# Moving the convolution's transposes of a gated-DeltaNet mixer from TensorE to VectorE and DRAM

## The chip, the cores and the metric

The kernel runs on one core of one Trainium2 chip. The metric is the device time of one execution in microseconds; the time before is the median of three runs. One further execution was taken with the hardware profiler, and all rows of the profile come from it.

## The reference

One decoder layer over 256 tokens of width 2048, in float32. Before and after a mixer stands a half-step SwiGLU FFN (width 5632), then a gated per-layer embedding and a last RMSNorm. The change lies in the mixer:

```python
proj = n @ w_in                       # q|k|v|z (1024 each), a, b, and q|k|v of the other 8 heads
qkv = silu(causal_depthwise_conv(proj[..., :3072], conv_w))     # 4 taps along time
q_c, k_c, v_c = split(qkv, 3)                                   # 8 heads of 128 each
q_c = l2_norm(q_c) * 128 ** -0.5;  k_c = l2_norm(k_c)           # over each head's 128 columns
o_dn = chunk_gated_delta_rule(q_c, k_c, v_c, g, beta)           # chunks of 64 tokens
o_dn = rms_norm(o_dn, dn_out_norm) * silu(z_dn)
o_sb = stick_breaking_attention(q_sb, k_sb, v_sb)
h = h + concat(o_dn, o_sb) @ w_out
```

The delta rule solves a unit lower triangular system for each head and chunk and then sweeps the chunks in order.

## The kernel before

**Matmuls.** Every float32 weight tile is loaded by SP into `raw` (four buffers of 128x1024, a pair of 128x512 tiles), rounded by ScalarE to `whi` (L68) and its remainder put by VectorE into `wlo` (L69), three buffers each. A product is three matmuls, hi*hi, hi*lo and lo*hi (L103 to L105), so a pair is twelve matmuls over the two halves of 128 tokens. `next_weights` keeps two pairs split ahead of the one in use.

**The mixer.** The input projection goes through fourteen blocks of 512 columns, in the order `W_IN_ORDER`, eight weight pairs each (112 pairs in all), and the output projection through four blocks. Blocks 2, 3 are k of the two head groups (four heads each), 0, 1 are q, 4, 5 are v; 8 to 13 belong to the attention and 6, 7 are z. A block's result (`pj`, two PSUM tiles, tokens on the partitions) is scaled by ScalarE into SBUF (`nat`, L663).

**Order of the work.** Side work is written as generators in three lanes. After each weight pair `lanes.step()` advances the first generator of every lane to its next `yield`: CONV holds the convolutions one after another, and later the attention's transposes and the gates; CHAIN holds the decays and then the delta rule of each head group; STICK the attention. Within this program order a planner in the framework may let an instruction of an engine go ahead of a blocked one; each engine then runs its queue in order. SP's queue holds the weight loads and the side work's transfers together.

**The convolution** (`conv_silu`) needs channels on the partitions and time along the row. `transpose_pair` turns `nat` on TensorE into PSUM (`tr_p`, L672, eight 128x128 transposes a block); ScalarE multiplies by the last tap (L801), VectorE adds the three others (L803) and ScalarE applies SiLU. `transpose4` (L679) turns the result back (`tr_b`, eight a block), and from PSUM ScalarE copies v (L818), or squares and sums q and k for their norms (`rnorm`, L785), GpSimd takes the power, and for k VectorE scales (L831); four transposes for each half of the tokens turn the scaled k again (`tr_kn`). The head group's chain starts its products `kk` (L876) when all three of its blocks are done (`ready`).

**The chain** (`chain`) forms `kk`, sends the diagonal blocks through DRAM, solves 32 rows one after another on VectorE (L904 and L906, dependent on each other), sends the solution back through DRAM, and runs some ten short products on TensorE, the last being `op1` (L956 into `op`), one step of the lane apart. Norms and a power follow; `gate` multiplies by SiLU of z, transposes, and makes `dnT`, the output projection's input. The second head group's `dnT` is used from the seventh pair of the first output block on.

**The other way to transpose** is there already (`transposed`, L163 to L177): VectorE transposes 32x32 blocks of a 128x512 tile, twice; SP stores both to a DRAM scratch tile (`scr`) and loads them with the block rows and columns exchanged, in four loads. It serves the norms' blocks, the FFN's inner activations, the attention's q and k, and the gate. It yields four times: after the block transposes, after the stores, after the loads, and once more.

Of the kernel before, what the change touches and what calls it, by code (L numbers as in the profile page):

```python
# [16 lines left out]
P = 128  # L17
# [13 lines left out]

W_IN_ORDER = (2, 0, 4, 3, 1, 5, 8, 10, 12, 9, 11, 13, 6, 7)
EPS = 1e-6
# [4 lines left out]
def block_kernel(ctx, tc, a, out):  # L38
# [14 lines left out]

    lanes = Lanes(3)
    dr = ctx.enter_context(tc.tile_pool(name="dr", bufs=1, space=bass.MemoryType.DRAM))
# [95 lines left out]
    def split_scaled(hi, lo, src, gain):  # L151
        nc.scalar.activation(hi, src, AF.Copy, scale=gain)
        nc.vector.scalar_tensor_tensor(out=lo, in0=src, scalar=gain, in1=hi.bitcast(F32),  # L153
                                       op0=ALU.mult, op1=ALU.subtract)

    def transposed(src, dst=None):

        scr = dr.tile([P, 2, 4, P], F32, tag="scr", name="scr", bufs=2)  # L160
        tmp = [act.tile([P, 4, P], F32, tag="nat", name="tb", bufs=4) for _ in range(2)]
        for t in range(2):
            nc.vector.transpose(tmp[t].rearrange("p c (j x) -> p c j x", j=4),  # L163
                                src(t).rearrange("p (j c x) -> p c j x", j=4, c=4))
        yield
        for t in range(2):
            nc.sync.dma_start(out=scr[:, t], in_=tmp[t])
        yield
        if dst is None:
            dst = [act.tile([P, 4, P], F32, tag="nat", name="tT", bufs=4) for _ in range(2)]  # L170
        for c in range(4):
            part = slice(32 * c, 32 * c + 32)
            if isinstance(dst, list):
                for t in range(2):
                    nc.sync.dma_start(out=dst[t][part], in_=scr[:, t, c, :].rearrange("(q x) i -> x q i", q=4))
            else:
                nc.sync.dma_start(out=dst[part], in_=scr[:, :, c, :].rearrange("(q x) t i -> x t q i", q=4))  # L177
        yield
        yield
        return dst  # L180

    def norm_block_behind(nT, which, j, tmp):

        hi, lo = nT
        yield
        tT = tmp()
        yield from transposed(lambda t: h[:, t, block(j)], tT)
# [30 lines left out]
    def block(j):  # L218
        return slice(j * NB, (j + 1) * NB)
# [178 lines left out]
    def ffn(n, nT, r, scale, next_norm, stat):  # L398
        xs = picker(*nT)
        late = callable(r)  # L400
        with tc.tile_pool(name="ffn", bufs=1) as fp:
            hTh, hTl = [], []

            def down_input(u, sil, th, tl):
                for t in range(2):
                    nc.vector.scalar_tensor_tensor(out=sil[:, t, :], in0=u[t], scalar=r[:, t:t + 1], in1=sil[:, t, :],
                                                   op0=ALU.mult, op1=ALU.mult)
                yield
                tT = fp.tile([P, 2, 4, P], F32, tag="tT", name="tT")
                yield from transposed(lambda t: sil[:, t, :], tT)  # L410
# [208 lines left out]
def mixer(tc, nc, a, act, mm_ps, mx_ps, accumulate, picker, new_nT, norm_block, sumsq, block, lanes, transposed,  # L619
          nT, r, h, stat, ident, mhalf):  # L620
    xs = picker(*nT)
    C64 = P // 2
    CONV, CHAIN, STICK = 0, 1, 2
    blocks = list(W_IN_ORDER)

    with tc.tile_pool(name="mix", bufs=1) as mp, \
# [32 lines left out]
        def to_sbuf(o, dst=None):  # L659
# [5 lines left out]
            return res  # L665

        def transpose_pair(nat, pr):

            tr = mx_ps("tr_p")
            for q in range(2):  # L670
                for t in range(2):
                    nc.tensor.transpose(tr[:, q * T + t * P:q * T + (t + 1) * P],  # L672
                                        nat[t][:, (2 * pr + q) * P:(2 * pr + q + 1) * P], ident)
            return tr

# [115 lines left out]

        def conv_silu(nat, part, hg):
            y = mp.tile([P, 4 * T + P], F32, tag="cT", name="cT", bufs=3)[:, 0:4 * T]
            trp = [transpose_pair(nat, pr) for pr in range(2)]
            for pr in range(2):
                for q in range(2):
                    c = 2 * pr + q
                    x = trp[pr][:, q * T:(q + 1) * T]
                    yc = y[:, c * T:(c + 1) * T]
                    w = conv[:, part * H + hg * 4 + c, :]  # L800
                    nc.scalar.activation(yc, x, AF.Copy, scale=w[:, 3:4])  # L801
                    for s in (1, 2, 3):
                        nc.vector.scalar_tensor_tensor(out=yc[:, s:], in0=x[:, 0:T - s], scalar=w[:, 3 - s:4 - s],  # L803
                                                       in1=yc[:, s:], op0=ALU.mult, op1=ALU.add)
                    yield
            if part == 0:
                yv = y.rearrange("p (c t x) -> p c t x", c=4, t=2)
                for t in range(2):
                    nc.scalar.activation(knq[hg][t][:, :, 1, :], yv[:, :, t, :], AF.Silu)
                src = lambda c, t: knq[hg][t][:, c, 1, :]  # L810
            else:
                nc.scalar.activation(y, y, AF.Silu)
                src = lambda c, t: y[:, c * T + t * P:c * T + (t + 1) * P]
            yield
            trs = [transpose4("tr_b", lambda c: src(c, t)) for t in range(2)]
            if part == 2:
                for t in range(2):
                    nc.scalar.copy(vn_[hg][:, t], trs[t])  # L818
            else:
                ss = mp.tile([P, 8], F32, tag="ss", name="ss", bufs=2)  # L820
                for t in range(2):
                    rnorm(trs[t], ss, t)
                if part == 0:
                    inv_sqrt(ss, rq[hg])
                else:
                    inv_sqrt(ss, ss)
                    yield
                    yield
                    kns = [kdec[hg], s2("kn1")]
                    for t in range(2):  # L830
                        nc.vector.tensor_tensor(out=v3(kns[t]), in0=v3(trs[t]), in1=bc(ss[:, t * 4:t * 4 + 4]),  # L831
                                                op=ALU.mult)
                    yield
                    yield
                    for t in range(2):
                        tr = transpose4("tr_kn", lambda c: kns[t][:, c * P:(c + 1) * P])
                        nc.scalar.copy(knq[hg][t][:, :, 0, :], v3(tr))
            ready[hg] += 1
            yield

        def dn_block(part, hg):
            nat = to_sbuf(natural(2 * part + hg))
            lanes.add(CONV, conv_silu(nat, part, hg))

# [5 lines left out]
        def chain(hg):  # L850
# [51 lines left out]
            for i in range(1, 32):  # L902
# [3 lines left out]
                nc.vector.tensor_reduce(out=sol[:, :, i:i + 1], in_=pm[:, :, 0:i + 1], axis=AX.X, op=ALU.add)  # L906
                if i % 4 == 3 or i % 2 and lanes.q[CONV]:
                    yield
# [80 lines left out]
            nc.vector.tensor_tensor(out=o[:, 1], in0=op1, in1=o[:, 1], op=ALU.add)  # L989


            coef = mp.tile([P, 8], F32, tag="coef", name="coef", bufs=2)
            for t in range(2):
                rnorm(o[:, t], coef, t)
            nc.vector.tensor_tensor(out=coef, in0=coef, in1=rq[hg], op=ALU.mult)
# [19 lines left out]
        def sb_transposed(nat, dst, part, hg):  # L1015

            if part == 0:
                parts = yield from transposed(lambda t: nat[t])
                qv = dst.rearrange("p (c t q y) -> p t q c y", c=4, t=2, q=4)
                for t in range(2):  # L1020
                    nc.scalar.copy(qv[:, t], parts[t].rearrange("p q (c y) -> p q c y", c=4))
            else:
                yield from transposed(lambda t: nat[t], dst.rearrange("p (t q x) -> p t q x", t=2, q=4))
            sb_ready[hg] += 1
# [78 lines left out]
        def gate(y, hg):  # L1103
            while not chain_done[hg]:
                yield
            for t in range(2):
                nc.vector.tensor_tensor(out=y[t], in0=y[t], in1=o_nat[hg][:, t], op=ALU.mult)
            yT = mp.tile([P, 4 * T + P], F32, tag="cT", name="yT", bufs=3)[:, 0:4 * T] \
                .rearrange("p (t q x) -> p t q x", t=2, q=4)
            yield from transposed(lambda t: y[t], yT)  # L1110
            if hg == 0:
# [101 lines left out]
```

## Time and profile before

| what | value |
|---|---|
| median of 3 runs | 1981.55 us (1981.34 to 1981.57) |
| the profiled execution's own time | 1982.68 us |
| its span, first to last instruction | 1981.0 us |
| mean granted TensorE clock | 0.999 |
| DMA moved | 421.64 MB, mean 213 GB/s |

The span covers the instructions; the 1.7 us between it and the execution's time lie around them. In rows of the profile, L numbers are lines of the kernel, a tile is written `out<-in`, and `128x512 f32` is partitions by elements. The input projection's matmuls start between 708 and 1085 us. PE is TensorE, DVE VectorE, ACT ScalarE, POOL GpSimd, and SPq the queue of SP's transfers.

### The profile page before, as it was taken

The numbers are of one execution on the slowest core, as the hardware profiler recorded it, in microseconds if no ns is written. First come the engines' busy times: TensorE is split into PE (matmuls) and PEld (weight loads), VectorE is DVE, ScalarE is ACT, GpSimd is POOL, SyncE is SP. The second block draws the span as 40 slices with busy tenths as digits, with TensorE's granted clock in tenths as the row PEclk, the third lists the DMA queues.
The fourth block names the chain that finished last, engine by engine and source line by source line (L and its number), as shares of the span: only waits on it lengthen the run. The fifth ranks groups of instructions, "written<-read, shape, count | busy, mean of one in ns | idle before, by whom it ended". The sixth has DMA issues, their size and how long they took to land. (4 is left out here: it accounts for less than half of the span.)

```text
span 1981.0 us, 24832 instructions
## 1 busy us (share of the span) xinstructions
PE 1961.9 (99%) x9022; PEld 1621.5 (82%) x9022; DVE 1507.4 (76%) x1803; ACT 1116.1 (56%) x1441; POOL 30.1 (2%) x46
## 2 busy tenths in 40 slices
PE   9999999999999999999999999999999999999998
PEld 7888888888888888878878888888888888888887
DVE  6878788777887766794786677888787877887655
ACT  6655555555555557654545455665565555655654
POOL 0000000000000000000100000000000000000000
PEclk9999999999999999999999999999999999999999
DMA  9666667756667665555564786665667656665764
GB/s 329 225 222 212 217 209 227 237 186 212 230 215 226 203 210 163 175 179 193 171 206 148 248 269 209 228 230 195 215 217 245 213 192 210 225 225 198 241 206 151
DMA packets 163228, 421.64 MB, mean 213 GB/s; under 512 B 20512, under 2 KB 59424, under 8 KB 162976
## 3 DMA queue, kind: packets, MB, share of 16 engines
q1 hardware_dynamic: 161952, 418.58, 64.2%
q10 hardware_dynamic: 1152, 1.47, 0.2%
q8 instruction: 71, 1.16, 0.2%
q14 instruction: 53, 0.43, 0.1%
HBM read 397.96 MB, written 22.02 MB: 212 GB/s over the span
## 5 line engine op out<-in xcount | busy, mean ns | idle before, releaser
L68 ACT CAST whi<-raw 128x1024 fp32r<-128x1024 f32 (+1 forms) x585 | 614.5, 1052 | 716.8 <-PE u L447 168.4
L69 DVE TENSOR_TENSOR wlo<-raw,whi 128x1024 fp32r<-128x1024 f32 (+1 forms) x585 | 711.9, 1220 | 372.0 <-ACT whi L68 370.9
L446 PE MATMUL g<-wlo,nTh 128*128 128x512 f32 x552 | 216.0, 391 | 0.4 <-DVE wlo L69 0.4
L445 PE MATMUL g<-whi,nTh 128*128 128x512 f32 x552 | 215.2, 391 | 0.7 <-ACT whi L68 0.7
L447 PE MATMUL g<-whi,nTl 128*128 128x512 f32 x552 | 215.8, 391 | 0.0
L445 PE MATMUL u<-whi,nTh 128*128 128x512 f32 x552 | 214.7, 389 | 0.0
L446 PE MATMUL u<-wlo,nTh 128*128 128x512 f32 x552 | 214.7, 389 | 0.0
L447 PE MATMUL u<-whi,nTl 128*128 128x512 f32 x552 | 214.7, 389 | 0.0
L445 PE MATMUL d<-whi,hTh 128*128 128x512 f32 x512 | 199.1, 389 | 1.0 <-ACT hTh L414 1.0
L446 PE MATMUL d<-wlo,hTh 128*128 128x512 f32 x512 | 199.2, 389 | 0.0
L447 PE MATMUL d<-whi,hTl 128*128 128x512 f32 x512 | 199.2, 389 | 0.0
L278 DVE TENSOR_TENSOR slo<-R,shi 128x1024 fp32r<-128x1024 f32 x155 | 189.3, 1222 | 12.6 <-ACT shi L277 2.7
L277 ACT CAST shi<-R 128x1024 fp32r<-128x1024 f32 x155 | 163.3, 1054 | 34.7 <-PE d L313 14.2
L103 PE MATMUL pj<-whi,nTh 128*128 128x512 f32 x448 | 179.5, 401 | 0.0
L104 PE MATMUL pj<-wlo,nTh 128*128 128x512 f32 x448 | 176.0, 393 | 2.3 <-DVE wlo L69 2.1
L105 PE MATMUL pj<-whi,nTl 128*128 128x512 f32 x448 | 175.3, 391 | 0.0
L446 PEld LDWEIGHTS g<-wlo,nTh 128*128 128x128 f32 x552 | 104.0, 188 | 23.7 <-DVE wlo L69 2.1
L445 PEld LDWEIGHTS g<-whi,nTh 128*128 128x128 f32 x552 | 104.0, 189 | 22.6 <-ACT whi L68 1.0
L447 PEld LDWEIGHTS g<-whi,nTl 128*128 128x128 f32 x552 | 104.0, 188 | 21.9 <-DVE nTl L153 0.4
L447 PEld LDWEIGHTS u<-whi,nTl 128*128 128x128 f32 x552 | 103.6, 188 | 21.6
L446 PEld LDWEIGHTS u<-wlo,nTh 128*128 128x128 f32 x552 | 103.6, 188 | 21.5
L445 PEld LDWEIGHTS u<-whi,nTh 128*128 128x128 f32 x552 | 103.6, 188 | 21.5
(301 smaller groups left out, 3028.3 us busy)
## 6 DMA issues: line engine op xcount, KB each, us to landing
raw<-in_w_gu SPq DMA_DIRECT2D x275, 512.0 KB, 4.2
raw<-in_w_down SPq DMA_DIRECT2D x128, 512.0 KB, 3.7
raw<-in_w_in SPq DMA_DIRECT2D x112, 512.0 KB, 3.6
R<-in_w_gu SPq DMA_DIRECT2D x76, 512.0 KB, 5.4
R<-in_w_down SPq DMA_DIRECT2D x48, 512.0 KB, 5.6
scr<-tb SPq DMA_DIRECT2D x74, 256.0 KB, 4.0
raw<-in_w_out SPq DMA_DIRECT2D x32, 512.0 KB, 4.2
raw<-in_w_pg SPq DMA_DIRECT2D x32, 512.0 KB, 4.4
```

Of the source, the lines that this page charges most:

```text
L68: nc.scalar.copy(hi[:, j, :], raw[:, j, :])
L69: nc.vector.tensor_tensor(out=lo[:, j, :], in0=raw[:, j, :], in1=hi[:, j, :], op=ALU.subtract)
L103: nc.tensor.matmul(outs[t], xh[:, c], whi[:, j, :], start=st, stop=False)
L104: nc.tensor.matmul(outs[t], xh[:, c], wlo[:, j, :], start=False, stop=False)
L105: nc.tensor.matmul(outs[t], xl[:, c], whi[:, j, :], start=False, stop=sp)
L277: nc.scalar.copy(hi, w)
L278: nc.vector.tensor_tensor(out=lo, in0=w, in1=hi, op=ALU.subtract)
L445: nc.tensor.matmul(out, xh[:, c], whi[:, j, :], start=st, stop=False, skip_group_check=True)
L446: nc.tensor.matmul(out, xh[:, c], wlo[:, j, :], start=False, stop=False, skip_group_check=True)
L447: nc.tensor.matmul(out, xl[:, c], whi[:, j, :], start=False, stop=sp, skip_group_check=True)
```

## The change

The forward and backward transposes of the convolution go through `transposed`; `tr_kn`, the chain's and the attention's own transposes stay on TensorE. The convolution reads and writes SBUF tiles: a first move brings `nat` into `y`, ScalarE copies it into `x` with the channels' four heads apart (two copies), the taps go from `x` to `y` as before, SiLU is applied, and a second move brings the result back into `x`, from which the norms, the copy of v and the scaling of k read. The blocks of a head group come as k, v, q, and they go into three lanes in turn (CONV and two new ones that are advanced after CHAIN and STICK). q counts as ready after its SiLU; the sum of its squares is needed by the chain's output norm, which waits for `rq_done`.

```diff
-W_IN_ORDER = (2, 0, 4, 3, 1, 5, 8, 10, 12, 9, 11, 13, 6, 7)
+W_IN_ORDER = (2, 4, 0, 3, 5, 1, 8, 10, 12, 9, 11, 13, 6, 7)
...
-    lanes = Lanes(3)
+    lanes = Lanes(5)
...
-        def rnorm(tr, ss, t):
+        def rnorm(src, ss, t):
             for c in range(4):
                 junk = act.tile([P, NB], F32, tag="junk", name="junk", bufs=1)
-                nc.scalar.activation(junk[:, 0:P], tr[:, c * P:(c + 1) * P], AF.Square,
-                                     accum_out=ss[:, t * 4 + c:t * 4 + c + 1])
+                x = src(c)
+                nc.scalar.activation(junk[:, 0:P].rearrange("p (q y) -> p q y", q=4) if len(x.shape) == 3 else
+                                     junk[:, 0:P], x, AF.Square, accum_out=ss[:, t * 4 + c:t * 4 + c + 1])
...
         def conv_silu(nat, part, hg):
+            x = mp.tile([P, 4 * T], F32, tag="sb", name="cx", bufs=6)
             y = mp.tile([P, 4 * T + P], F32, tag="cT", name="cT", bufs=3)[:, 0:4 * T]
-            trp = [transpose_pair(nat, pr) for pr in range(2)]
...
+            yield from transposed(lambda t: v3(nat[t]), y.rearrange("p (t q x) -> p t q x", t=2, q=4))
+            yv = y.rearrange("p (t q c y) -> p t q c y", t=2, q=4, c=4)
+            xv = x.rearrange("p (c t q y) -> p t q c y", c=4, t=2, q=4)
+            for t in range(2):
+                nc.scalar.copy(xv[:, t], yv[:, t])
+            yield
+            for c in range(4):
+                xc, yc = x[:, c * T:(c + 1) * T], y[:, c * T:(c + 1) * T]
...
+                yield
             if part == 0:
                 for t in range(2):
-                    nc.scalar.activation(knq[hg][t][:, :, 1, :], yv[:, :, t, :], AF.Silu)
-                src = lambda c, t: knq[hg][t][:, c, 1, :]
+                    nc.scalar.activation(knq[hg][t][:, :, 1, :], yv[:, t], AF.Silu)
+                src = lambda t: knq[hg][t][:, :, 1, :]
+                ready[hg] += 1
...
             yield
-            trs = [transpose4("tr_b", lambda c: src(c, t)) for t in range(2)]
+
+            back = x.rearrange("p (t q x) -> p t q x", t=2, q=4)
+            yield from transposed(src, back)
...
                 if part == 0:
                     inv_sqrt(ss, rq[hg])
+                    rq_done[hg] = True
+                    return
...
         def dn_block(part, hg):
             nat = to_sbuf(natural(2 * part + hg))
-            lanes.add(CONV, conv_silu(nat, part, hg))
+            lanes.add(CONVS[len(turns) % 3], conv_silu(nat, part, hg))
+            turns.append(part)
...
-                if i % 4 == 3 or i % 2 and lanes.q[CONV]:
+                if i % 4 == 3 or i % 2 and any(lanes.q[x] for x in CONVS):
                     yield
...
+            while not rq_done[hg]:
+                yield
...
-            for part in (1, 0, 2):
+            for part in (1, 2, 0):
                 dn_block(part, hg)
```

`CONVS = (0, 3, 4)`; `turns` counts the blocks. The other callers of `transposed` pass the same data in a view of three dimensions instead of two.

More of the change, by code (lines that the diff above doesn't have):

```diff
@@ L154, in split_scaled, with by_four @@
                                        op0=ALU.mult, op1=ALU.subtract)
+    def by_four(x):
+        return x.rearrange("p (j i) -> p j i", j=4)
     def transposed(src, dst=None):
@@ L186, in norm_block_behind @@
         tT = tmp()
-        yield from transposed(lambda t: h[:, t, block(j)], tT)
+        yield from transposed(lambda t: by_four(h[:, t, block(j)]), tT)
         for kk in range(4):
@@ L409, in down_input @@
                 tT = fp.tile([P, 2, 4, P], F32, tag="tT", name="tT")
-                yield from transposed(lambda t: sil[:, t, :], tT)
+                yield from transposed(lambda t: by_four(sil[:, t, :]), tT)
                 for t in range(2):
@@ L665, in to_sbuf @@
             return res
[L667 to L674, printed above, removed]
         def transpose4(name, src):
@@ L792, in conv_silu @@
         def conv_silu(nat, part, hg):
+            x = mp.tile([P, 4 * T], F32, tag="sb", name="cx", bufs=6)
             y = mp.tile([P, 4 * T + P], F32, tag="cT", name="cT", bufs=3)[:, 0:4 * T]
-            trp = [transpose_pair(nat, pr) for pr in range(2)]
[L795 to L805, printed above, removed]
+            yield from transposed(lambda t: v3(nat[t]), y.rearrange("p (t q x) -> p t q x", t=2, q=4))
@@ new lines, in conv_silu @@
+            yv = y.rearrange("p (t q c y) -> p t q c y", t=2, q=4, c=4)
[5 more added lines that the diff above has]
+                xc, yc = x[:, c * T:(c + 1) * T], y[:, c * T:(c + 1) * T]
+                w = conv[:, part * H + hg * 4 + c, :]
+                nc.scalar.activation(yc, xc, AF.Copy, scale=w[:, 3:4])
+                for s in (1, 2, 3):
+                    nc.vector.scalar_tensor_tensor(out=yc[:, s:], in0=xc[:, 0:T - s], scalar=w[:, 3 - s:4 - s],
+                                                   in1=yc[:, s:], op0=ALU.mult, op1=ALU.add)
+                yield
@@ L817, in conv_silu @@
                 for t in range(2):
-                    nc.scalar.copy(vn_[hg][:, t], trs[t])
+                    nc.scalar.copy(vn_[hg][:, t].rearrange("p (c q y) -> p q c y", c=4, q=4),
+                                   x.rearrange("p (t q c y) -> p t q c y", t=2, q=4, c=4)[:, t])
             else:
@@ L821, in conv_silu @@
                 for t in range(2):
-                    rnorm(trs[t], ss, t)
+                    rnorm(lambda c: back[:, t, c], ss, t)
                 if part == 0:
                     inv_sqrt(ss, rq[hg])
[L825 to L837, printed above, removed]
+                    rq_done[hg] = True
+                    return
+                inv_sqrt(ss, ss)
+                yield
+                yield
+                kns = [kdec[hg], s2("kn1")]
+                for t in range(2):
+                    nc.vector.tensor_tensor(out=kns[t].rearrange("p (c q y) -> p c q y", c=4, q=4), in0=back[:, t],
+                                            in1=ss[:, t * 4:t * 4 + 4].rearrange("p (c o z) -> p c o z", o=1, z=1)
+                                            .broadcast_to([P, 4, 4, 32]), op=ALU.mult)
+                yield
+                yield
+                for t in range(2):
+                    tr = transpose4("tr_kn", lambda c: kns[t][:, c * P:(c + 1) * P])
+                    nc.scalar.copy(knq[hg][t][:, :, 0, :], v3(tr))
             ready[hg] += 1
             yield
+        rq_done = [False, False]
+        turns = []
         def dn_block(part, hg):
             nat = to_sbuf(natural(2 * part + hg))
-            lanes.add(CONV, conv_silu(nat, part, hg))
+            lanes.add(CONVS[len(turns) % 3], conv_silu(nat, part, hg))
+            turns.append(part)
         o_nat = [mp.tile([P, 2, NB], F32, tag="onat", name="onat", bufs=2) for _ in range(2)]
@@ L1017, in sb_transposed @@
             if part == 0:
-                parts = yield from transposed(lambda t: nat[t])
+                parts = yield from transposed(lambda t: v3(nat[t]))
                 qv = dst.rearrange("p (c t q y) -> p t q c y", c=4, t=2, q=4)
@@ L1022, in sb_transposed @@
             else:
-                yield from transposed(lambda t: nat[t], dst.rearrange("p (t q x) -> p t q x", t=2, q=4))
+                yield from transposed(lambda t: v3(nat[t]), dst.rearrange("p (t q x) -> p t q x", t=2, q=4))
             sb_ready[hg] += 1
@@ L1109, in gate @@
                 .rearrange("p (t q x) -> p t q x", t=2, q=4)
-            yield from transposed(lambda t: y[t], yT)
+            yield from transposed(lambda t: v3(y[t]), yT)
             if hg == 0:
```

11 lines of the change are left out of this document (7 added, 4 removed).

## Prediction, made before the changed kernel was run

> **What bounds the kernel now.** I read the page's busy times first, then the windows of the mixer, then the waits there, then single engines in order of time.
>
> ```profile
> span 1981.0 us, 24832 instructions
> PE 1961.9 (99%) x9022; PEld 1621.5 (82%) x9022; DVE 1507.4 (76%) x1803; ACT 1116.1 (56%) x1441; POOL 30.1 (2%) x46
> ```
>
> TensorE is busy for 99% of the span, so an instruction taken off it is worth its time, provided that the weights still come in time. The windows of the mixer say where that proviso is tight (columns: stretch, length, then busy us of each engine, granted clock, DMA share, GB/s):
>
> ```profile
> core 0: us, PE busy (x) PEld busy (x) DVE busy (x) ACT busy (x) POOL busy (x), PEclk, DMA share, GB/s
> 735.00:817.00 82.00, 80.77 (x398) 67.40 (x396) 52.71 (x97) 58.82 (x102) 4.55 (x4) 1.00 0.53 168
> 817.00:890.00 73.00, 71.62 (x337) 58.60 (x336) 67.39 (x138) 41.29 (x79) 4.18 (x2) 1.00 0.58 177
> 890.00:942.00 52.00, 52.00 (x356) 43.45 (x355) 25.17 (x29) 24.97 (x43) 1.32 (x1) 1.00 0.61 200
> ```
>
> The convolutions fill the first two windows. In the second VectorE is busy for 67.39 of 73.00 us, beside TensorE's 71.62; in the third it has half its time free. So TensorE bounds the kernel everywhere, and from 817 to 890 VectorE is close behind. The waits of the mixer (total us, times, longest) agree:
>
> ```profile
> ACT whi L68 <- PE pj L105: 111.5, 64, 4.0
> PE pj L104 <- DVE wlo L69: 2.1, 4, 0.9
> PE tr_b L679 <- ACT cT L812: 1.2, 1, 1.2
> ```
>
> The cast of the weights waits for TensorE to give a buffer back (111.5 us), hardly ever the other way round (2.1 us). The third row is a backward transpose for which TensorE stood idle until the SiLU was done.
>
> **What the change removes.** Each of the six convolution blocks loses eight forward transposes (tr_p) and eight backward ones (tr_b).
>
> ```profile
> L672 PE MATMUL tr_p<-ident,nat x48: 270/272/273, 738.2 to 876.6; 128*128 128x128 f32 x48
> L679 PE MATMUL tr_b<-ident,cT x32: 271/273/327, 756.2 to 891.1; 128*128 128x128 f32 x32
> L679 PE MATMUL tr_b<-ident,knq x16: 270/272/273, 788.4 to 870.3; 128*128 128x128 f32 x16
> ```
>
> That is 48 + 32 + 16 = 96, in twelve groups of eight. The 272 ns are a pipelined duration; what a group takes from the projection shows in TensorE's order of time:
>
> ```profile
> 887.63 0.39 PE L103 MATMUL pj<-whi,nTh 128*128 128x512 f32 x1
> ...
> 890.12 0.39 PE L105 MATMUL pj<-whi,nTl 128*128 128x512 f32 x1
> 890.36 1.03 PE L679 MATMUL tr_b<-ident,cT 128*128 128x128 f32 x8
> 891.15 0.48 PE L103 MATMUL pj<-whi,nTh 128*128 128x512 f32 x1
> 891.46 0.39 PE L104 MATMUL pj<-wlo,nTh 128*128 128x512 f32 x1
> ```
>
> From 887.63 to 890.12 lie twelve matmuls, eleven steps, so one takes 0.227 us and a pair of weight tiles (twelve matmuls) 2.72 us. From 890.12 to 891.46 are two steps, 0.45 us without the group, but 1.34 us went by: a group costs 0.88 us. Twelve make 10.6 us, and the 1.2 us wait for the SiLU goes with them. Gross: **-11.8 us**.
>
> **What it adds on VectorE.** Twelve moves of two 128x512 block transposes. The convolution's multiply-adds stay, now reading SBUF. The groups of the stretch from 817 to 890 (count, busy us, mean ns, idle before and what ended it), and one such pair of block transposes:
>
> ```profile
> L68 ACT CAST whi<-raw 128x1024 fp32r<-128x1024 f32 x23 | 24.2, 1051 | 25.3 <-PE pj L105 24.3 <-ACT cT L801 1.0
> L69 DVE TENSOR_TENSOR wlo<-raw,whi 128x1024 fp32r<-128x1024 f32 x24 | 29.1, 1214 | 2.2 <-ACT whi L68 2.1
> L803 DVE SCALAR_TENSOR_TENSOR cT<-tr_p,conv,cT 128x255 f32<-128x255 f32 (+2 forms) x36 | 14.8, 472 | 0.0
> L904 DVE TENSOR_TENSOR pm<-sol,L 128x16 f32<-128x16 f32 (+30 forms) x31 | 12.8, 411 | 0.9
> L906 DVE TENSOR_REDUCE sol<-pm 128x8 f32<-128x16 f32 (+30 forms) x31 | 9.2, 295 | 0.9
> L831 DVE TENSOR_TENSOR kdec<-tr_b,ss 128x512 f32<-128x512 f32 x1 | 0.7, 692 | 1.6 <-POOL ss L790 1.6
> 888.66 1.30 DVE L163 STREAM_TRANSPOSE tb<-nat 128x512 f32<-128x512 f32 x2
> ```
>
> A move costs VectorE 1.3 us, twelve 15.6 us. Seven fall before the first head group's kk products, where 82.00 - 67.40 = 14.6 us are free: I cost those at nothing. The other five (k backward, v both ways, q both ways, second group) fall into the stretch of the first triangular solve, whose 62 instructions take 22 us. TensorE's time for that stretch shrinks by six groups and its idle 1.4 us, 73.0 - 5.3 - 1.4 = 66.3 us. VectorE needs 67.4 + 5 x 1.3 = 73.9, and 1.6 more where it stands waiting for GpSimd's power (the kdec row), 75.5 us: short by 9.2 us. What cushions it: three sets of split weights, so TensorE has two pairs (5.4 us) in hand while a new one takes 1.05 + 1.21 = 2.3 us, which leaves 3.1 us; and I let 1 us slip into the light stretch after it (q's backward move is needed only by the output norm). 9.2 - 4.1 = 5.1 us of waiting, against 1.4 now: **+3.7 us**. Bounds: -1.4 (all absorbed) and 9.2 + 4.0 (the other idle time of VectorE there, 5.6 - 1.6) - 1.4 = +11.8.
>
> A rule stands against this exchange. The Trainium skill (VectorE: DVE Perf Modes, Rules for kernel authors) says to transpose 128x128 on TensorE if a PSUM destination will do, and calls VectorE's own transpose the fastest for 32x32 blocks only. By that rule VectorE's side of the exchange would be the dearer one; it is the third rival.
>
> **On ScalarE, SP and the queues.**
>
> ```profile
> L1021 ACT COPY sb<-tT x4: 616/618/632, 898.9 to 986.1; 128x512 f32<-128x512 f32 x4
> L167 SPq DMA_DIRECT2D scr<-tb x74: 320/327/1584, 59.5 to 1861.8; - x74
> L177 SPq DMA_DIRECT2D yT<-scr x8: 568/609/614, 1062.2 to 1096.9; - x8
> ACT sb L1021: 0.9, 1
> SPq L167 <- DVE tb L163: 15.6, 12, 3.0
> SPq L177 <- DMA scr<-tb: 7.5, 5, 2.7
> ACT whi L68 <- DMA raw<-in_w_in: 6.4, 3, 5.1
> ```
>
> ScalarE gets twelve copies of 0.62 us, 7.4 us in 155 us of which it is busy 58.82 + 41.29 = 100: nothing. Each copy waits for its transfer with the casts of the weights queued behind it; of the four like it one waited, 0.9 us, under the 3.1 us in hand. Behind it the order of waits is cast, VectorE's subtraction, matmul. SP issues per move two stores (0.33) and four loads (0.61), 3.1 us, and stands in order behind each block transpose and each store's landing, with the next weight loads behind it: at most 3.0 + 2.7 + 3.1 = 8.8 us. The third window holds two such moves and shows TensorE busy for 52.00 of 52.00 us, so I take 0; bounds 0 and +6 (three waits as long as the worst shown, 5.1, less 3.1).
>
> **On the chain of the delta rule.** Lanes advance one step per weight pair, so the yields can be counted. Before, k, q, v take 11, 7 and 7 steps one after another from pair 9 on, and the first group is ready at pair 32. Now k starts at 9, v at 17, q at 25; q's tenth step at 34 makes it ready, and since its lane comes after the chain's, the chain sees it at 35. The first chain ends three pairs later, so the second starts at 77, not 74. Its solve meets a busy convolution lane at other places and wins one pair back: its last product op1 stands after pair 111, not 109, of 112. What follows op1 has no slack today:
>
> ```profile
> L105 PE MATMUL pj<-whi,nTl x448: 387/389/580, 708.9 to 1085.2; 128*128 128x512 f32 x150
> 1076.37 1.05 PE L956 MATMUL op<-vn,AT 128*128 128x128 f32 x8
> 1090.62 0.33 SPq L167 DMA_DIRECT2D scr<-tb  x1
> 1094.92 2.54 SPq L177 DMA_DIRECT2D yT<-scr  x4
> 1100.25 1.14 ACT L1118 CAST dnT<-yT 128x512 fp32r<-128x512 f32 x2
> 1101.75 0.39 PE L103 MATMUL wo<-whi,dnT 128*128 128x512 f32 x1
> DVE zg L1107 <- ACT zg L1137: 1.8, 2, 1.0
> ```
>
> The projection ends at 1085.2 + 0.2 = E. op1 stood at E - 9.0 (three pairs and its own group); now E - 3.6. From op1 to the cast are 23.9 us, through norms, gate, store and load; the cast's first half takes 0.6. That makes E + 20.9, less 1.0 us in which the gate waited for the last z block's SiLU (last row), which now is done before op1's follow-up: E + 19.9. TensorE wants it at 1101.75 = E + 16.3: **+3.6 us**. Bounds: two pairs, 5.4; and 0.9 if the planner puts one pair of the next output block (2.72) into the gap. [...]
>
> **Sum.** -11.8 + 3.7 + 3.6 = -4.5 us against the profiled execution's 1982.68 us (span 1981.0 and 1.7 around it). The median of the runs, 1981.55, lies 1.1 lower; the same difference gives **1977.0 us**.
>
> **The rivals.** Full gain: VectorE catches up by working ahead (in the solve the planner already runs it ahead of the pairs), and one pair covers the gap at the output projection: -11.8 - 1.4 + 0.9 = -12.3, 1969.3 us. For it speaks the free half of the third window; against it, 9.2 us must be found in 66.
>
> Cancelled: VectorE's shortage comes through nearly whole, +11.8, with the tail's 3.6: +3.6, 1985.1 us. For it: instructions of VectorE run in order, and the solve's steps stand ahead of later pairs' subtractions.
>
> Slower, VectorE the bound over both windows: if the first seven moves find their 14.6 us of idle time in the wrong places (it sits where VectorE waits for ScalarE's cast), all 15.6 us lie on the path: -11.8 + 15.6 + 3.6 = +7.4, 1989.0 us. It decides once the added work exceeds what is idle plus 3.1 us of weights in hand. Rows for: 1.30 us a move against 0.88 us a group on TensorE. Against: the cast waits 111.5 us for TensorE. The Trainium skill's rule above would be right here.
>
> Slower by the queue: SP's 8.8 us hold makes weights late. With half of the twelve moves costing 2.0 (5.1 - 3.1): +12 on my sum, 1989 us. Against it: the third window.
>
> **How the numbers follow.** Some 0.2% (4 us) is what a measurement here can tell from no change. My forecast has 0.45; its own range is 1973 to 1981, two thirds of it faster (0.30), the rest within (0.15). Full gain 0.20, faster. Cancelled 0.17, of it 0.12 within and 0.05 slower. VectorE the bound 0.11 and the queue 0.07, slower. Faster 0.50, same 0.27, slower 0.23. The range reaches from 1969.5 (full gain) to 1987.0 (past the cancelled case), leaving the two slower rivals out.
>
> **What would show it.** No tr_p or tr_b on TensorE; 24 more block transposes of 0.65 to 0.7 us; TensorE waiting for wlo some 5 us during the first solve (right), none (full gain) or over 10 (cancelled); TensorE idle 2 to 5 us before the first wo matmul on dnT's second group. I am wrong if ScalarE's cast waits for raw by more than 10 us in the mixer, or if the first wait appears before 817 us.

## The result, and the profile after

The changed kernel takes 2010.42 us (median of 4 runs, 2008.68 to 2011.69) against 1981.56 for the kernel before (4 runs): a ratio of 1.0145, 95% interval [1.0128, 1.0163]. It is 28.9 us slower; the forecast was 4.5 us faster, and the range ended at 1987.0. The profiled execution took 2011.36 us. The page's span and busy times, and then the windows of the mixer (the prediction's stretches and columns):

```profile
span 2009.6 us, 24808 instructions
PE 1960.1 (98%) x8926; PEld 1615.6 (80%) x8926; DVE 1522.9 (76%) x1827; ACT 1120.9 (56%) x1452; POOL 28.6 (1%) x46
```
```profile
735.00:817.00 82.00, 75.82 (x334) 60.40 (x332) 56.84 (x104) 55.61 (x88) 3.09 (x3) 0.98 0.70 218
817.00:890.00 73.00, 58.69 (x236) 46.82 (x237) 63.85 (x130) 35.50 (x71) 3.28 (x2) 0.88 0.73 220
890.00:942.00 52.00, 44.89 (x293) 36.13 (x292) 26.72 (x38) 25.13 (x47) 0.00 (x0) 0.97 0.66 195
```

The edit is as announced: 96 matmuls fewer, 24 instructions of VectorE more, 15.5 us. But from 817 to 890 TensorE is busy for 58.69 us instead of 71.62, VectorE for less than before, and the granted clock is 0.88. No engine is full; they wait for each other. The waits from 735 to 960, first TensorE's and ScalarE's, then SP's queue in the changed kernel, and last SP's queue in the kernel before:

```profile
PE pj L103 <- ACT whi L68: 16.1, 5, 7.0
PE pj L104 <- DVE wlo L69: 7.3, 7, 3.6
ACT whi L68 <- PE pj L105: 38.6, 22, 3.1
ACT nat L667 <- PE pj L105: 18.6, 8, 5.3
ACT cT L812 <- DVE cT L802: 7.3, 1, 7.3
```
```profile
SPq L65 <- DVE wlo L69: 60.9, 27, 10.9
SPq L170 <- DVE tb L166: 36.6, 22, 6.9
SPq L180 <- DMA scr<-tb: 12.6, 10, 4.2
```
```profile
SPq L65 <- DVE wlo L69: 134.0, 53, 6.6
```

TensorE now waits for the weights' cast. ScalarE waits for TensorE (`nat`) and VectorE (SiLU) instead of having casts ready. On SP's queue a weight load used to stand waiting for a free buffer for 134.0 us of this stretch: that was the slack of the weight stream. Now it is 60.9, and the moves' stores and loads stand there for 36.6 + 12.6 = 49.2 us. An engine's queue can stand still behind one instruction that waits, with ready ones behind it; I call that a hold. One of them, on ScalarE and on VectorE:

```profile
863.60 0.31 ACT L781 ACTIVATE junk<-cx 128x128 f32<-128x128 f32 x1
863.82 0.19 ACT L781 ACTIVATION_READ_ACCUMULATOR junk<-cx 128x1 f32 x1
871.28 1.06 ACT L812 ACTIVATE cT<-cT 128x1024 f32<-128x1024 f32 x1 [7.28 <-DVE cT L802]
...
872.53 1.03 ACT L68 CAST whi<-raw 128x1024 fp32r<-128x1024 f32 x1
```
```profile
865.43 0.60 DVE L914 TENSOR_TENSOR pm<-sol,L 128x232 f32<-128x232 f32 x1
866.07 0.40 DVE L916 TENSOR_REDUCE sol<-pm 128x8 f32<-128x232 f32 x1
866.38 4.80 DVE L802 SCALAR_TENSOR_TENSOR cT<-cx,conv,cT 128x255 f32<-128x255 f32 x12
```

All twelve taps of a block stand behind the solve's rows on VectorE, the SiLU stands behind the taps, the next cast behind the SiLU (its weights had landed at 864.5 us), and TensorE is without a product for 7 us. Measured by the start of the same weight pair, the changed kernel leads by 6.0 us at pair 25 (779.7 against 785.7), trails by 16.9 at pair 49 and by 27.7 at pair 65, and by 17 to 28 from there on.

### The profile page after: what moved, and what is told of

Same layout as the page of the kernel before. It is cut to its first block, busy times and chain, and to the rows that moved or that the text cites. A ratio compares the mean times of both kernels' runs of the same rounds, so it can differ in the third digit from the quotient of the medians.

```text
span 2009.6 us, 24808 instructions
## 1 busy us (share of the span) xinstructions
PE 1960.1 (98%) x8926; PEld 1615.6 (80%) x8926; DVE 1522.9 (76%) x1827; ACT 1120.9 (56%) x1452; POOL 28.6 (1%) x46
## 4 chain that ended last, share of the span: by engine, by line
PE 49%; DVE 3%; DMA 1%; issue 1%; ACT 1%; SPq 0%; POOL 0%; ACTq 0%; POOLq 0%; DVEq 0%
PE g L448 3%; PE u L449 3%; PE g L450 3%; PE g L449 3%; PE u L450 3%; PE u L448 3%; PE d L450 3%; PE d L448 3%; PE d L449 3%; PE pj L104 2%; PE pj L105 2%; PE pj L103 2%; PE wo L104 1%; PE wo L105 1%; PE wo L103 1%; DVE wlo L69 1%
## 5 line engine op out<-in xcount | busy, mean ns | idle before, releaser
L281 DVE TENSOR_TENSOR slo<-R,shi 128x1024 fp32r<-128x1024 f32 x155 | 189.2, 1222 | 12.6 <-ACT shi L280 2.9
```

The source lines that it names most:

```text
L281: nc.vector.tensor_tensor(out=lo, in0=w, in1=hi, op=ALU.subtract)
```

## Experiments

Each label has a short edit. A time without a range is a single run, which stands beside a run of the kernel before on the same chip (1981.5 to 1983.0 us).

**Parts of the change alone.** `e1_lanes_only` keeps the three lanes, the order k, v, q and the early `ready`, with all transposes on TensorE. `e4_forward_moved` moves the forward transposes only, `e5_backward_moved` the backward ones only. `e2_extra_transposes` adds the 24 block transposes to the kernel before; it leaves nothing out.

```diff
 e2: in three added lanes, twice a block
+                for t in range(2):
+                    nc.vector.transpose(xv[:, t]..., h[:, t, 0:NB]...)      # nothing reads xv
```

> The changed kernel's three lanes, its order k, v, q and q's early readiness, with all 96 transposes back on TensorE. Theory (ScalarE's queue: the SiLU stands ahead of the weights' casts and waits for taps of the convolution that come late because they follow a transfer and are bunched): no transfers in the convolution, so 1978 to 1986 us. Rival lanes (three blocks at once make the bunching by themselves): 2000 us or more. Rival load (VectorE's 24 more block transposes): 1978 to 1986. Rival transfers: 1978 to 1986.

> The kernel before with 24 more 128x512 block transposes on VectorE, four a block, ten steps between a block's two pairs as in the changed kernel, whose results nobody reads; the 96 transposes stay on TensorE. It adds VectorE's load of the change without its dependences and transfers. Rival load: all of the loss or more, 2005 to 2020 us, most of it while the first solve runs. Theory (ScalarE's queue): 1981 to 1990. Rival transfers, rival lanes: 1981 to 1988.

> The changed kernel with the backward transposes on TensorE; the forward ones stay on VectorE and DRAM. Theory (ScalarE's queue): the taps still follow a transfer and come in a bunch, so most of the loss stays: 1998 to 2012 us, SiLU waiting for taps for several us each. Rival load (half of the block transposes): 1990 to 2000. Rival transfers (half): 1990 to 2000.

> The changed kernel with the forward transposes on TensorE; the backward ones stay on VectorE and DRAM. Theory (ScalarE's queue): the taps are paced by TensorE's transposes again and the SiLU waits as little as before, so little of the loss stays: 1976 to 1988 us. Rival load (half of the block transposes): 1990 to 2000. Rival transfers (half): 1990 to 2000.

1982.60, 1981.60, 1982.77 and 1979.34 us. None is slower than the kernel before; the lanes cost nothing, and my theory's 1998 to 2012 for e4 was wrong. Six moves are not free: they take six groups of 0.88 us off TensorE, 5.3 us by the prediction's price, and e4 shows 0.2 of it and e5 3.6. But all twelve lose 28.9 us, far more than the two halves together.

e2 tests less than its expectation says. Its block transposes wait for nothing, and all 24 ran before the first solve; from 817 to 890 VectorE is busy for 67.42 us there, as in the kernel before (67.39). The run that has them at the change's pace is e18, further down. The rows of both:

```profile
L848 DVE STREAM_TRANSPOSE cx<-h x24: 668/671/706, 717.8 to 753.1; 128x512 f32<-128x512 f32 x24
L850 DVE STREAM_TRANSPOSE tb<-h x24: 666/701/717, 733.2 to 894.6; 128x512 f32<-128x512 f32 x24
```

**Placing ScalarE's instructions.** My next theory was the hold shown above: SiLU ahead of the casts.

```diff
 e6
+            with tc.issue_after(lanes.cast):          # the newest weight cast
                 nc.scalar.activation(y, y, AF.Silu)
 e7: the same around every step of the three convolution lanes
 e8
-            for i in range(1, 32):
+            for i in range(31, 32):                   # rows 1 to 30 of each solve left out
 e9
-    CONV, CHAIN, STICK = 0, 1, 2;  CONVS = (0, 3, 4)
+    CONV, CHAIN, STICK = 0, 3, 4;  CONVS = (0, 1, 2)
```

> The full change; only the convolution's SiLU (L808, L812) is queued on ScalarE behind the newest weight cast. Theory A (ScalarE takes its queue in order, and a SiLU that waits for the taps on VectorE holds the casts behind it): the three longest SiLU waits of after (7.28, 4.39 and 4.07 us) and the slow clock behind them go, so 1985 to 1998. Rival B (VectorE has too little time beside the triangular solve, wherever ScalarE's instructions stand): 2004 to 2012. Rival C (the twelve round trips through DRAM delay the weights): 2004 to 2012.

> The full change; every ScalarE instruction of the convolution's three lanes (copies, first taps, SiLU, squares) is queued behind the newest weight cast that was written before it. Theory A: no cast stands behind a convolution's instruction that waits, so nearly all of the 28 us goes: 1974 to 1988. Rival B (VectorE too full beside the solve): casts are in time, but their low halves come late from VectorE all the same: 1998 to 2012. Rival C (transfers): 2004 to 2012.

> The full change with rows 2 to 31 of both triangular solves left out, so the attention output is not that of the reference: some 45 us less of VectorE in short instructions. Theory A says the taps wait behind solve rows in VectorE's queue, and the SiLU and the casts behind the taps; without the rows the taps come at once: 1972 to 1985. Rival B (VectorE's load): the same 1972 to 1985. Rival C (transfers): still 2000 to 2012.

> The full change with the delta rule's chain as the last but one of the five lanes instead of the second, so that at each step the three convolution lanes come ahead of the solve's rows in program order. Theory A in its stricter form (it is the taps of the second and third lane, written behind the solve's rows, that come late): 1980 to 1998. If the order of the lanes does not matter to what the queues get: 2004 to 2012. Rival B and C: 2004 to 2012.

2025.49, 2017.03, 1989.48, 2012.99 us. (e8 leaves out rows 1 to 30 and keeps the last; its expectation names them 2 to 31.) Moving the SiLU made it worse: that hold was a symptom, and other instructions took its place. Without the solve's rows 20.9 us go (2010.42 - 1989.48), so the solve seems to have a part in the loss, but e8 does not price VectorE's load alone: the yields between the rows go too, the first chain's z stands at pair 51 instead of 61, and the kernel before without these rows was not run.

Counting ScalarE's instructions in order then gave a pattern. Before, and in e1, e4 and e5, each of the eight copies of a projection out of PSUM stands behind the casts of the next block's first two pairs. In the changed kernel it stands ahead of both at three ends of blocks, in e6 and e7 at five. Four runs on that:

```diff
 e11 (e12: with e7's edit too)
+                with tc.issue_after(lanes.cast):
                     nc.scalar.activation(s, o[t], AF.Copy, scale=r[:, t:t + 1])
 e13: the kernel before, casts of two pairs queued behind that copy at three ends of blocks
 e3: the kernel before, in three added lanes, twice a block
+                yield from transposed(lambda t: h[:, t, 0:NB], xv)          # nothing reads xv
```

> The full change; only the copy of each projection out of PSUM (L667) is queued on ScalarE behind the newest weight cast. Counted in the traces, that copy stands behind the casts of the next block's first two pairs at all eight ends of blocks before, with either half alone, and with the lanes alone; in the full change it stands ahead of both at three of them (the fourth, seventh and eighth block), and in the two slower variants at five. Theory D (it is this place in ScalarE's queue, since the copy can't run before the block's last product, and the two casts wait behind it): three to five us for each of three places and what they start, 1975 to 1992. Rival B (VectorE too full beside the solve): 2000 to 2012. Rival C (the round trips through DRAM): 2004 to 2012.

> The full change with both the copy out of PSUM (L667) and every ScalarE instruction of the convolution's lanes queued behind the newest weight cast. Theory D: the paced kernel was slower only because its copy stood ahead of the casts at five ends of blocks; now at none, so 1970 to 1985, and no slower than the copy alone. Rival B: 2000 to 2015. Rival C: 2004 to 2015.

> The kernel before, nothing of the change in it, with the casts of the next block's first two pairs put behind the copy out of PSUM at the ends of the fourth, seventh and eighth block, as the full change has it. Theory D: each place holds TensorE for the copies, one cast and one subtraction less what overlaps, three to five us, with the slow clock behind it: 1991 to 2004. Rivals B and C: the queue's order costs nothing by itself while VectorE and the transfers are as before: 1980 to 1986.

> The kernel before with twelve whole moves added whose result nothing reads: 24 block transposes on VectorE and their 24 writes and 48 reads by DRAM on SyncE's queue, at the pace of the change. It leaves nothing out. Theory D: the moves by themselves cost nothing, unless they too put the copy ahead of the casts: 1979 to 1988. Rival C (the round trips take the weights' bandwidth or place in the queue): 1995 to 2012.

2007.34, 1999.65, 1983.66 and 2020.56 us. The copy's place costs 0.7 us by itself (e13), so that theory fell as well, though with e7's edit in place it is worth 17.4 us (2017.03 - 1999.65). But e3 hit: twelve whole moves, added to a kernel that keeps all its transposes on TensorE, cost 37.6 us. It is the moves, whatever TensorE does.

**What of a transfer.** e17 keeps the bytes but lets no DMA wait for anything new; e18 keeps the number and the waits with a sixteenth of the bytes or less; e15 is the full change with the moves on GpSimd's queue; e19 has six scratch tiles.

```diff
 e15 (in the convolution's two calls)
-        nc.sync.dma_start(...)
+        nc.gpsimd.dma_start(...)
 e17
+                    nc.sync.dma_start(out=scr[:, t], in_=h[:, t, 0:NB]...)   # twelve scr
+                    nc.sync.dma_start(out=xv[part], in_=scr0[:, :, c, :]...) # written once
 e18
+                    nc.sync.dma_start(out=scr[:, t, 0, 0:32], in_=tmp[t][:, 0, 0:32])
 e19
-        scr = dr.tile([P, 2, 4, P], F32, tag="scr", name="scr", bufs=2)
+        scr = dr.tile([P, 2, 4, P], F32, tag="scr", name="scr", bufs=6)
```

> The full change; only the queue of the convolution's twelve moves is another, GpSimd's instead of SyncE's. Bytes, buffers, transposes and lanes stay. Theory E (on SyncE's queue, taken in order, the writes wait for VectorE's transposes and the reads for the writes, and the weight loads stand behind them): 1970 to 1988. Theory F (the bytes themselves, 12 MB in some 200 us, slow the weight loads): 2000 to 2014. Theory G (two scratch buffers in DRAM and four of the nat buffers are too few for three blocks): 2000 to 2014.

> The kernel before with the same 24 transposes, 24 writes and 48 reads added as in the extra moves (2020.56 us), but no DMA waits for anything new: the writes take a finished tile, into twelve scratch buffers, and the reads a scratch tile written once at the start. It leaves nothing out. Theory E (waits on the queue): 1980 to 1990. Theory F (bytes): 2000 to 2022. Theory G (buffers): 1980 to 1988.

> The kernel before with the extra moves' transposes, waits and number of DMAs, but each DMA moves a sixteenth or less (32 elements of each row). It leaves nothing out. Theory E: the waits are there, somewhat shorter since small transfers land sooner: 1990 to 2015. Theory F: 1979 to 1986. Theory G: buffers are held for less time: 1980 to 1995.

> The full change with six scratch buffers in DRAM instead of two for all moves. Theory G: a write no longer waits for the reads of the move two before: 1980 to 1998. Theory E: only a part of the waits on the queue goes, 1998 to 2011. Theory F: 2004 to 2014.

1993.31, 2006.04, 1984.28 and 2011.20 us. The scratch tiles do not matter. Another queue takes away 17.1 of the 28.9 us, and the weight loads have their slack back; SP's queue in e15, 735 to 960:

```profile
SPq L65 <- DVE wlo L69: 136.1, 49, 6.1
```

So most of the loss comes with the weights' queue. Whether by waits on the chip or by the order that was laid down, e15 does not tell apart: in its trace the copies stand behind the casts at all eight ends again, and its first chain is spread from pair 63 to 71. The bytes without new waits (e17) cost 24.5 us.

e18 has the moves' block transposes, though nothing reads their results, and their number of DMAs, and it costs 2.8 us (1984.28 - 1981.51), against 37.6 in e3: so neither VectorE's load nor the number of DMAs is dear, but the size of the transfers and what follows from it. On the waits e18 says less than I meant it to: its small transfers land sooner, and its DMAs waited for only 5.8 + 4.8 = 10.6 us, against 49.2 in the change (all moves of the stretch; in the kernel before, 8.9):

```profile
SPq L854 <- DVE tb L850: 5.8, 12, 2.4
SPq L857 <- DMA scr<-tb: 4.8, 5, 2.8
```

In e17 part of the loss is of a kind that the waits hide. TensorE's order of time, short products of the first chain and no projection between them:

```profile
926.20 1.14 PE L971 MATMUL t<-X,dec 64*64 64x64 f32 x16 [0.47 <-ACT X L964]
928.17 1.69 PE L977 MATMUL z<-Z,tw 64*64 64x64 f32 x16 [0.84 <-issue]
930.53 2.08 PE L984 MATMUL up<-v,Z 128*128 128x128 f32 x8 [0.67 <-ACT Z L978]
933.39 2.08 PE L984 MATMUL sp<-u,kdec 128*128 128x128 f32 x8 [0.78 <-DVE u L990]
935.26 1.92 PE L984 MATMUL op<-u,AT 128*128 128x128 f32 x8
```

Each is a link that waits for the one before. Counted in the traces, the chain from its first z to ks has five pairs of the projection spread through it in the kernel before (pairs 63 to 68); in e17 all of it stands at pair 63, in the changed kernel they stand from pair 61 to 64, but for the last of ks. The queues are run in the order in which they were filled (the cast shown above waited behind the SiLU with its weights landed), so this order was laid down when the kernel was built. The weights themselves were there: in the changed kernel ScalarE has no idle time from 735 to 960 that the landing of a weight tile ends. The bunched chain is not the whole of it: from pair 63 to 64 e17 falls back by 13.9 us against the kernel before, and 6.3 of them return by pair 70. In e5, the fastest of all, the same links stand from pair 61 to 62; it falls back by 8.5 us from pair 61 to 64, and 6.3 return by pair 72.

**Pinning the order.** Everything that a lane issues is queued behind the newest product on TensorE, the newest cast on ScalarE and the newest subtraction on VectorE; the copies out of PSUM stand behind the newest cast too.

```diff
 e21 (the full change), e24 (e17 with it)
-                next(self.q[lane][0])
+                with self.behind("product", "cast", "sub"):
+                    next(self.q[lane][0])
```

> The full change with the place of the lanes in the queues pinned: at each pair of weight tiles, whatever a lane issues is queued on TensorE behind the newest product, on ScalarE behind the newest cast and on VectorE behind the newest subtraction; the copies out of PSUM stand behind the newest cast too. In the full change's trace the first chain's products from t to ks stand with three pairs between them (pairs 61 to 64) instead of six (62 to 68), so that TensorE waits out each link. Theory H (the queues' orders, fixed when the kernel is built, treat the weights as late once many bytes are moved, and bring everything else forward ahead of them; on the chip the weights are in time): 1968 to 1982. Theory F (the bytes delay the weights on the chip): 1995 to 2012. Theory E (waits on SyncE's queue hold the weight loads on the chip): 1985 to 2005.

> The bytes without waits (2006.04 us) with the same pins; nothing of the change is in it, the extra transposes, writes and reads are. Theory H: the bytes cost only by the order that the queues were given, so 1979 to 1988. Theory F: 2000 to 2010, whatever the order. Theory E: 1979 to 1988 as well (no DMA waits for anything new).

e24: 1988.58 us (1987.56 to 1990.58), ratio 1.0034 [1.0023, 1.0046]. Pinned, the same bytes cost 7.2 us instead of 24.5, so some 17 of it look like order; the kernel before with the pins alone was not run, so what they do without the bytes is open. e21: 2005.19 us (2001.09 to 2010.04), 1.0117 [1.0102, 1.0133]: only 5 us better than the change, and my expectation missed. Its waits (in the profiled execution, the slowest of the five) show what the order had covered, first ScalarE's from 735 to 960, then SP's queue in order of time:

```profile
ACT whi L69 <- DMA raw<-in_w_in: 19.1, 9, 4.5
ACT junk L793 <- DMA cx<-scr: 9.3, 3, 7.8
```
```profile
821.29 1.41 SPq L66 DMA_DIRECT2D raw<-in_w_in  x2
823.17 2.54 SPq L182 DMA_DIRECT2D cT<-scr  x4
826.64 1.25 SPq L172 DMA_DIRECT2D scr<-tb  x2
831.74 1.80 SPq L911 DMA_DIRECT2D sc<-dec  x4
833.96 1.29 SPq L182 DMA_DIRECT2D cx<-scr  x2
835.41 0.56 SPq L915 DMA_DIRECT2D L<-sc  x1
836.02 1.26 SPq L182 DMA_DIRECT2D cx<-scr  x2
837.32 14.12 SPq L66 DMA_DIRECT2D raw<-in_w_in  x7
```

From 822.4 (the second of the two loads) to 837.3 no weight load is issued, 14.9 us, five and a half pairs of 2.72 us, while two moves and the chain's own transfers each wait for their source in the queue. The load issued then lands at 842.5, and TensorE's longest wait in this run, 5.5 us, ends at 844.8. By my estimate four `raw` buffers cover four pairs, 10.9 us. With six moves the longest such stretch is 8.9 us (e4) and 7.9 (e5), 7.0 in the kernel before, which the buffers cover. That fits the cheap halves and the dear whole, but no run has more buffers, so the threshold is not shown; and a long stretch can also be a result, as in the change, where the longest, 13.3 us from 862.1, is the hold shown above: the loads wait there for a free buffer.

**What is settled and what is not.** Settled: the moves' transfers are the cause (e3 against e18), and 17.1 of the 28.9 us come with their place on the weights' queue (e15). Likely, for want of the pins alone on the kernel before: a large part of what bytes do is done through the queues' order (e24). For the change itself two limits seem to lie one behind the other: with the order as built the weights wait in ScalarE's queue, with the order pinned they come late from SP's. Open: e15 is still 11.8 us above the kernel before and some 24 above the full gain. Its trace names TensorE waiting for the scaled k (8.3 us) and ScalarE for the moves' loads (9.4), neither tested, and the moves on GpSimd's queue with the order pinned were not run. Why the planner places the copies and the chain earlier when more bytes are moved was not shown. None of the versions beats the kernel before for certain; e5, at 1979.34 us in a single run beside 1982.93, is the best of them.

## Why the prediction was wrong, point by point

**Removal, -11.8: held where it could be seen.** By pair 25 three groups and the SiLU's wait were gone, 3 x 0.88 + 1.2 = 3.8 us by the prediction's terms, and the group of `tr_kn`, another 0.9, was only put off; the lead there is 6.0. After that holds cover it.

**VectorE, +3.7: its size came by luck.** TensorE waits for `wlo` from 817 to 890 for 4.8 us, where some 5 were forecast. But VectorE was not short over the stretch: it was busy for 63.85 of 73.00 us, and e18, with as many block transposes at the same pace, takes 2.8 us more than the kernel before. Most of the 4.8 us is one wait of 3.65 us:

```profile
843.26 0.79 PE L104 MATMUL pj<-wlo,nTh 128*128 128x512 f32 x1 [3.65 <-DVE wlo L69]
```
```profile
838.84 0.30 DVE L914 TENSOR_TENSOR pm<-sol,L 128x80 f32<-128x80 f32 x1
...
841.81 0.27 DVE L916 TENSOR_REDUCE sol<-pm 128x8 f32<-128x112 f32 x1
841.99 1.22 DVE L69 TENSOR_TENSOR wlo<-raw,whi 128x1024 fp32r<-128x1024 f32 x1
```

The cast for it was done at 838.8 us, itself late by a hold; its subtraction then stood behind ten instructions of the solve's rows. That is the argument of the rival "cancelled", the solve's steps ahead of later subtractions, but as an order in the queue and not as too little time. The Trainium skill's rule (VectorE: DVE Perf Modes, Rules for kernel authors), by which the transposes belong on TensorE, has the right sign here, but not by VectorE's price: e18 pays that price, and it is 2.8 us at most. One reading in the prediction was wrong too: the 14.6 us it calls free before the first kk products are 82.00 less 67.40, which is PEld's column. VectorE's is 52.71, so 29.3 us were free, and the rival that builds on the 14.6 was weaker than it says.

**ScalarE, SP and the queues, 0 with bounds 0 and +6: this step failed.** It took the third window, with two moves and TensorE full, for twelve moves in 200 us. From the removal of 11.8 us to the loss of 28.9 are 40.7 us; e15 shows that 17.1 of it come with the choice of queue alone, where the bounds allowed 6. The wait of a store for its transpose was taken as 3.0 us at most and of a load for its store as 2.7; they came to 6.9 and 4.2. And the working assumed that all queues keep their order but for what is added, which the counts refute. The rival "slower by the queue" named the place, at 0.07, and priced it at +12 on the sum.

**The tail, +3.6: +2.2.** From the projection's last product to the last of `wo` lie 1201.1 - 1111.9 = 89.2 us; before, 1172.4 - 1085.4 = 87.0. `op1` stands after pair 111, as forecast, and TensorE idles for 1.13 + 0.53 = 1.7 us, inside the bounds (idle before the product, and what ended it):

```profile
1129.58 0.73 PE L103 MATMUL wo<-whi,dnT 128*128 128x512 f32 x2 [1.13 <-ACT whi L68]
1130.84 0.50 PE L104 MATMUL wo<-wlo,dnT 128*128 128x512 f32 x1 [0.53 <-DVE wlo L69]
```

But the rows name a weight's cast and its remainder, and the second group's `dnT` is cast only from 1130.64 us on, with no idle time of TensorE behind it. So the size is near, and the wait that was forecast by name is not what the rows show; why the weight's cast came late was not looked into.

**What was to show it wrong.** One sign came: the first hold is before 817 us (1.1 us for `whi`, up to 787.95). The other did not: the cast does not wait for `raw` by 10 us, because it stands behind other instructions before the landing matters. A test by one named wait misses a delay that sits in the order of a queue.

## What to carry to other kernels

A transfer that waits for a result does not belong on the in-order queue that feeds the bottleneck; before moving work there, compare the longest stretch that the queue can be held with what the input buffers cover (here some 10.9 us, a sign and not a tested threshold), for all the moves that are in flight together and not for one. Six moves that cost some 2 to 5 us say little of twelve. Look in the trace when an added load really ran before trusting the run that adds it (e2). And when waits move elsewhere with each repair, count the order of the queues against the kernel before: how many casts stand ahead of a copy, how many pairs between two links of a chain.

## What the runs showed of the hardware

After a long hold TensorE runs at half its clock for a while. After 1.38 and 1.16 us of idle time the matmuls' starts lie 0.43 us apart instead of 0.23, for some 3.4 us (granted clock from 806 to 809: 0.51):

```profile
805.66 0.50 PE L104 MATMUL pj<-wlo,nTh 128*128 128x512 f32 x1 [1.16 <-DVE wlo L69]
806.00 0.55 PE L105 MATMUL pj<-whi,nTl 128*128 128x512 f32 x1
806.35 0.63 PE L104 MATMUL pj<-wlo,nTh 128*128 128x512 f32 x1
806.77 0.63 PE L105 MATMUL pj<-whi,nTl 128*128 128x512 f32 x1
807.20 0.63 PE L103 MATMUL pj<-whi,nTh 128*128 128x512 f32 x1
```

From 700 us on, 46 such steps in the changed kernel's projections, 0.2 us longer each, add 9.1 us, against 2.5 before. So up to 6.6 of the 28.9 us are not waiting but what waiting does to the clock, and the prediction had no term for it. The Trainium skill (TensorE: Matmul & The Clock Gate, Part 1: The HAM clock gate) gives half rate until some 3.4 us of sustained work have passed, and the stretch after this hold agrees; after the longest hold the slow steps last from 873.6 to 881.2 us, 7.6 us with 0.6 us of idle time in it. It names an idle window of as much as the trigger, and here 2.5 us in two pieces were enough, while 1.11 and 0.53 us at 788 were not (clock 1.00 from 787 to 792).
